# Low parts of the input weights: kept in DRAM after the first pass, loaded again in the second

## The chip, the core and the metric

The kernel runs on one core of one Trainium2 chip, as one program with one launch. Its time is the device time of one execution in microseconds, lower is better; for several executions the median is given. The core has TensorE (PE, matrix products; its weight loads are shown as PEld), VectorE (DVE), ScalarE (ACT), GpSimd (POOL), and SyncE (SP), whose queue issues every DMA of this kernel. Each engine works through its own instructions strictly in the order in which the program issues them, and waits on semaphores for the others.

## The reference, cut to what matters

One inference layer is computed for a prompt of 1024 tokens and for a sample group of 8 x 8 = 64 tokens, with the same weights and in float32:

```
proj = x @ w_in                                  # (tokens, 2048) x (2048, 6672)
conv:  u = glu_a * sigmoid(glu_b); depthwise causal conv, width 31; layer norm; silu; * silu(gate)
delta: q, k, v = silu(conv width 4); gated delta rule, 8 heads x 128, in chunks; rms norm; * silu(gate)
mem:   attention of 4 heads over 256 memory tokens; * silu(gate)
h = concat(conv, delta, mem) @ w_out             # (tokens, 2048) x (2048, 2048)
y = layer_norm(alpha * x + h)
```

The states of the two convolutions, of the delta rule and the memory's keys and values are outputs too.

## The kernel before

**Split products.** A float32 product is made of three fast products (type `fp32r`). A weight block of 128 x 512 arrives in `raw`. ACT copies it into `wh`, rounded to `fp32r`; another engine subtracts, `wl = raw - wh`; the activations are split in the same way into `xh` and `xl`; and PE adds up `wh*xh + wh*xl + wl*xh` in PSUM. One such pair `wh`, `wl` is called a split. `split_quarter` (L302) makes one, half of a `raw` tile, and the kernel makes 592 of them. Which engine subtracts is decided by the number of the split: every second one from the 10th to the 450th goes to POOL, the others to DVE. `wh` and `wl` have four slots each, so a split waits until PE is through with the pair made four splits before it.

**Passes.** `gemm` (L1229) computes one column block of 128 output channels, in four quarters of four contraction blocks; a quarter uses up one split. The first pass runs over 52 column blocks with 576 tokens (half of the prompt and the sample group, in two banks of 288); before block 44 `run_mem` (L1302) computes the memory's keys and values, with 32 splits of its own and, in `load_mem`, eight split activations. The second pass runs over the same 52 blocks and the same weights for the other 512 tokens: it loads them again and splits them again. Then come eight blocks of the output projection with layer norm ("the out stage"), with 144 splits. So the splits are numbered 1 to 240 in the first pass (177 to 208 for the memory), 241 to 448 in the second and 449 to 592 in the out stage.

**Order of the work.** The order of all instructions is written down when the program is made, by a planner. The class `Model` keeps a clock for each engine with a price for each instruction; `Side` holds generators for everything beside the big products: `gen_conv4`, `gen_k`, `gen_q`, `gen_v`, `gen_chain`, `gen_s` for a head of the delta rule (a "unit"), `gen_cgroup` and `gen_cln` for the wide convolution, `gen_att` for a memory head. `side.tick` is called between the products and lets each generator emit a step when its inputs are ready by the model's clock. `side.drain(cond)` emits side work, and no big product, until a condition no longer holds. `ensure(n)` makes splits until `n` of them are ready; it is called with 2 around each quarter.

**What PE may wait for.** In the program's order the subtraction of a split stands between steps of side work on the same engine, and PE takes a `wl` two quarters later.

**POOL's other work** in the passes: in `gen_k` four products of masks, each over 128 x 512 elements (`gmh`, `gml` = triangle times gates; `Dm` = `D` times triangle; `D` times `zn`), in `gen_s` the scaling of the state `S0` (twice) and `ux`, the three sums of `gen_cln`, small copies and powers.

**Work tiles.** Nineteen slots of the tag `W` and sixteen of `T5` hold the intermediate tiles. Nothing in the planner counts them: an instruction that writes a tile for which no slot is free waits on its engine.

**SP's queue.** `load_more` issues loads of `raw` (five slots, 512 KB each) in a fixed sequence; a `raw` slot is free when `done_raw(hi, lo)` says so, that is after the copy and the subtraction of its second half.

## Time and profile before

| what | value |
|---|---|
| median of 3 runs | 2069.68 us (2062.01, 2069.68, 2070.32) |
| the profiled execution | 2062.28 us, its span 2060.6 us |
| PE busy in the span | 1973.7 us (96%) |
| DVE, ACT, POOL busy | 1429.6, 844.7, 605.7 us |
| first pass, memory included | 0 to about 927 us |
| second pass | about 927 to 1649 us |
| out stage | about 1649 to 2060.6 us |
| share of time that the DMA queue's packets take | 36.5% of 16 engines |

The span runs from the first to the last instruction; what lies around it is 1.7 us. The stages are read off the first and last instructions that write the tiles of each stage. Almost all instructions carry the line of one helper (L86), so groups are told apart by the names of their tiles: `wl<-raw,wh` writes `wl` and reads `raw` and `wh`. A busy PE is not a PE at its peak, since matmuls overlap; what counts for the end is the time at which the next big product can start.

### The profile page before, as it was taken

The page shows a single profiled execution, that of the slowest core. Times are in us where ns is not written, and L with a number is a line of the kernel's source. Part 1 is how long each engine was busy: PE and PEld are TensorE (multiplying, and loading weights), DVE is VectorE, ACT ScalarE, POOL GpSimd, SP SyncE. Part 2 cuts the span into 40 slices and gives each one's busy share as a digit, 9 for nine tenths or more (in the row PEclk, how much of TensorE's full clock was granted, in tenths as well). Part 3 has the DMA queues.
Part 4 walks back from the last instruction along what each step waited for, and adds up shares of the span by engine and source line. Part 5 has one row for each costly group of instructions (what it writes and reads, how often), then busy time and mean ns, then how long its engine had stood idle before and what let it go on. Part 6 is the DMA issues. An engine that isn't in the chain of part 4 may idle for free. (4 is left out here: it accounts for less than half of the span.)

```text
span 2060.6 us, 33195 instructions
## 1 busy us (share of the span) xinstructions
PE 1973.7 (96%) x12156; PEld 1708.8 (83%) x12156; DVE 1429.6 (69%) x3190; ACT 844.7 (41%) x2013; POOL 605.7 (29%) x680
## 2 busy tenths in 40 slices
PE   8999999999999989999999999999989999999995
PEld 7999999999999969977777887787767788877784
DVE  7777877887789984255787776779985433348447
ACT  5444444444433345364444444443326522235124
POOL 6434333343323242113333333322322100006003
PEclk9999999999999999999999999999999999999998
DMA  5333233323233355354332223332232563345444
GB/s 205 93 100 93 88 96 102 102 82 99 86 99 97 104 165 167 109 176 149 96 93 89 76 89 104 102 93 82 90 102 92 156 205 105 106 159 182 141 132 144
DMA packets 107267, 239.50 MB, mean 116 GB/s; under 512 B 32224, under 2 KB 36576, under 8 KB 106848
## 3 DMA queue, kind: packets, MB, share of 16 engines
q1 hardware_dynamic: 107104, 237.39, 36.5%
q8 instruction: 95, 1.56, 0.3%
q14 instruction: 68, 0.56, 0.1%
HBM read 210.24 MB, written 27.10 MB: 115 GB/s over the span
## 5 line engine op out<-in xcount | busy, mean ns | idle before, releaser
L86 PE MATMUL m<-xh,wh 128*128 128x288 f32 (+1 forms) x2496 | 860.4, 345 | 7.4 <-ACT wh L86 7.4
L86 PE MATMUL m<-xh,wl 128*128 128x288 f32 (+1 forms) x2496 | 820.1, 329 | 12.7 <-DVE wl L86 9.6
L86 PE MATMUL m<-xl,wh 128*128 128x288 f32 (+1 forms) x2496 | 816.9, 327 | 0.0
L86 ACT CAST wh<-raw 128x512 fp32r<-128x512 f32 x592 | 359.5, 619 | 396.4 <-PE om L86 220.7
L86 POOL TENSOR_TENSOR wl<-raw,wh 128x512 fp32r<-128x512 f32 x221 | 308.5, 1396 | 725.5 <-ACT wh L86 695.5
L86 PEld LDWEIGHTS m<-xh,wh 128*128 128x128 f32 x2496 | 471.0, 189 | 54.3 <-issue 14.1
L86 PEld LDWEIGHTS m<-xh,wl 128*128 128x128 f32 x2496 | 469.7, 188 | 54.3 <-DVE wl L86 14.8
L86 PEld LDWEIGHTS m<-xl,wh 128*128 128x128 f32 x2496 | 471.4, 189 | 29.9 <-issue 2.4
L86 DVE TENSOR_TENSOR wl<-raw,wh 128x512 fp32r<-128x512 f32 x371 | 283.8, 771 | 265.9 <-ACT wh L86 265.5
L86 DVE SCALAR_TENSOR_TENSOR hc<-u,cvc,hc 128x512 f32<-128x512 f32 x360 | 241.5, 713 | 3.1
L86 PE MATMUL om<-wl,xh 128*128 128x512 f32 x576 | 226.8, 394 | 11.6 <-DVE wl L86 10.5
L86 PE MATMUL om<-wh,xh 128*128 128x512 f32 x576 | 226.9, 394 | 4.2 <-ACT wh L86 2.9
L86 PE MATMUL om<-wh,xl 128*128 128x512 f32 x512 | 200.7, 392 | 0.0
L86 DVE TENSOR_TENSOR xt<-mb,X 128x8 f32<-128x8 f32 (+30 forms) x496 | 182.3, 368 | 12.0 <-DVE mb L650 0.3
L86 DVE SCALAR_TENSOR_TENSOR cv<-xr,qcw,cv 128x512 f32<-128x512 f32 (+1 forms) x216 | 167.1, 774 | 7.7
L86 POOL TENSOR_TENSOR y<-y,lnb 128x512 f32<-128x512 f32 (+1 forms) x32 | 51.7, 1639 | 341.7 <-DVE y L86 222.6
L86 PEld LDWEIGHTS om<-wl,xh 128*128 128x128 f32 x576 | 108.9, 189 | 38.8 <-DVE wl L86 14.9
L86 ACT ACT_TABLE_LOAD x89 | 114.2, 1283 | 46.7 <-DVE smz L86 25.8
L86 PEld LDWEIGHTS om<-wh,xh 128*128 128x128 f32 x576 | 109.1, 189 | 29.1 <-ACT wh L86 4.6
L86 DVE TENSOR_REDUCE X<-xt 128x4 f32<-128x8 f32 (+30 forms) x496 | 110.1, 222 | 10.6
L86 PEld LDWEIGHTS om<-wh,xl 128*128 128x128 f32 x512 | 97.1, 190 | 20.2
L86 ACT ACTIVATE oi<-ps,GT 128x128 f32<-128x128 f32 x56 | 20.6, 367 | 207.8 <-DVE r L86 192.7
(309 smaller groups left out, 2010.1 us busy)
## 6 DMA issues: line engine op xcount, KB each, us to landing
raw<-in_wt_dram SPq DMA_DIRECT2D x208, 512.0 KB, 3.8
raw<-in_wo_dram SPq DMA_DIRECT2D x72, 512.0 KB, 3.8
mb<-ysc SPq DMA_DIRECT2D x128, 64.0 KB, 2.2
raw<-mx SPq DMA_DIRECT2D x16, 512.0 KB, 3.8
xt<-in_xp_dram SPq DMA_DIRECT2D x32, 256.0 KB, 4.4
out_y_p_dram<-y SPq DMA_DIRECT2D x32, 256.0 KB, 2.6
xraw<-in_xa_dram SPq DMA_DIRECT2D x16, 288.0 KB, 5.4
S<-in_sdelta_dram SPq DMA_DIRECT2D x16, 256.0 KB, 4.6
```

What stands on the lines that cost most here:

```text
L86: r = fn(**kw)
```

## The change

It does these things:

- In the first pass every `wl` but those of the memory's weights is also written to a DRAM tile of its own (`lop`, 208 of 256 KB); the write is issued by SP one split later.
- In the second pass `wl` isn't computed: after ACT's copy, SP issues a load of the DRAM tile into the `wl` slot. `raw` is then free after ACT's copy alone.
- All other subtractions are on DVE; POOL makes none.
- Five slots for `wh` and `wl` instead of four (`WB`), and `ensure(3)` in `gemm` and `run_mem` instead of `ensure(2)`; the out stage keeps 2 but for its last phase.
- The masks leave POOL: `gmh`, `gml`, `Dz`, `S0` and `ux` are made on ACT, four instructions of 128 columns each (`rscale`). The product `Dm` goes away; in its place PE adds a matrix of -30000 below the diagonal to the exponent (`identr` x `negr`, 512 columns, one for each of 16 units), before ACT's `Exp`.
- The planner counts the slots of `W` and `T5`: generators wait in `room` and `room5` until slots are free (one is kept back for the oldest unit, `fleet[0]`), `need` drains side work until a slot is free, and `finish` drains until the only `xr` buffer has been read (`xbusy`). The sum of squares in `gen_cln` is made with two tiles instead of five. `T5` has 17 slots, the small `Z` tiles 12.
- `xh` and `xl` share one tile.

```diff
+WB = 5
+KEEP = 1
...
-    NW, NX, NU, N5, NZ = 19, 1, 2, 16, 8
+    NW, NX, NU, N5, NZ = 19, 1, 2, 17, 12
...
+    def room(n, last=None):
+        while wfree[0] < n + (0 if last is None or last() else KEEP):
+            yield "B"
+        wfree[0] -= n
...
+    def need(n=1):
+        side.drain(lambda: wfree[0] < n)
...
     def split_quarter():
...
+        n = nsplit[0]
         nsplit[0] += 1
...
         act.copy(out=hi, in_=s)
-        eng = pool if (nsplit[0] % 2 == 0 and 8 < nsplit[0] <= 450) else dve
-        eng.tensor_tensor(out=lo, in0=s, in1=hi.bitcast(F32), op=ALU.subtract)
+        again = n - len(lop) - 32
+        if 0 <= again < len(lop):
+            sp.dma_start(out=lo.bitcast(F32), in_=lop[again])
+        else:
+            dve.tensor_tensor(out=lo, in0=s, in1=hi.bitcast(F32), op=ALU.subtract)
+        while keep and (len(keep) > 1 or keep[0][0] < n - 1 or n >= len(lop) + 32):
+            m, t = keep.popleft()
+            sp.dma_start(out=lop[m], in_=t.bitcast(F32))
+        slot = n if n < 176 else n - 32
+        if n < 176 or 208 <= n < 240:
+            lop[slot] = drp.tile([P, 512], F32, name=f"lo{slot}")
+            keep.append((slot, lo))
...
-            done_raw(hi, lo)
+            done_raw(hi, *(() if 0 <= again < len(lop) else (lo,)))
...
+    def rscale(out, srcs, scales):
+        for c, (x, s) in enumerate(zip(srcs, scales)):
+            act.activation(out=out[:, c, :], in_=x, func=AF.Identity, scale=s)
...
     def gen_k(u):
-        pool.tensor_tensor(out=gmh, in0=bc(triu), in1=bl(gt["gh"][:, 0:4, h].bitcast(F32), 4, P), op=ALU.mult)
-        pool.tensor_tensor(out=gml, in0=bc(triu), in1=bl(gt["gl"][:, 0:4, h], 4, P), op=ALU.mult)
+        yield from room(2, lambda: fleet[0] is u)
+        rscale(gmh, [triu] * 4, [gt["gh"][:, c, h:h + 1].bitcast(F32) for c in range(4)])
+        rscale(gml, [triu] * 4, [gt["gl"][:, c, h:h + 1] for c in range(4)])
...
+        pe.matmul(out=psD.rearrange("p (c n) -> p c n", c=4), lhsT=identr, rhs=bc(negr), start=False, stop=True)
...
-        pool.tensor_tensor(out=Dm, in0=D, in1=bc(triu), op=ALU.mult)
-        u["Dm"] = Dm
-        pool.tensor_tensor(out=D, in0=D, in1=bl(zn, 4, P), op=ALU.mult)
+        u["Dm"] = D
+        rscale(Dz, [D[:, c, :] for c in range(4)], [zn[:, c:c + 1] for c in range(4)])
...
     def finish(p, t, psl):
...
+            side.drain(lambda: xbusy[0])
+            xbusy[0] = 1
             xr, xs = evac_qkv(p, ci, psl)
...
     def gemm(p, t, prev_fin, xhook=None):
-            ensure(2)
+            ensure(3)
```

## The prediction, made before the changed kernel ran

> **What bounds the kernel now.** I read the page's busy times first, then what PE waited for, because PE is the only engine that is nearly full:

> ```profile
> span 2060.6 us, 33195 instructions
> PE 1973.7 (96%) x12156; PEld 1708.8 (83%) x12156; DVE 1429.6 (69%) x3190; ACT 844.7 (41%) x2013; POOL 605.7 (29%) x680
> ```

> The change takes no big product away, so it can only pay where PE stands still or runs slowly. The waits of PE up to 1645 us (both passes), then from 1649 us (the out stage), each as total, number of times and longest in us:

> ```profile
> PE mm L86 <- DVE wl L86: 10.6, 3, 4.6
> PE m L86 <- DVE wl L86: 9.6, 12, 1.7
> PE m L86 <- ACT wh L86: 7.4, 1, 7.4
> PE ps L86 <- DVE rbuf L86: 5.3, 9, 1.2
> PE ps L86 <- DVE S L86: 3.6, 4, 2.0
> PE m L86 <- POOL wl L86: 3.0, 4, 1.1
> PE ps L86 <- DVE ut L86: 2.4, 5, 0.5
> PE ps L86 <- ACT cv L86: 2.2, 2, 1.4
> PE ps L86 <- ACT bdT L86: 1.9, 1, 1.9
> ...
> PE ps L86 <- POOL lsum L86: 1.2, 1, 1.2
> ```

> ```profile
> PE om L86 <- DVE wl L86: 10.5, 6, 6.8
> PE om L86 <- ACT wh L86: 2.7, 1, 2.7
> ```

> The reader is to see how little there is. Late subtractions in the passes cost 10.6 + 9.6 + 3.0 = 23.2 us; side work adds some 17; the 7.4 is the start, and the 13.2 lie in the out stage, whose splits are on DVE before and after. The three waits at `mm` (the memory's products) cost more than themselves. The next table cuts the span where the granted clock fell; its columns are stretch, length, busy us (instructions) of PE, PEld, DVE, ACT, POOL, the granted clock, DMA share and GB/s:

> ```profile
> 720.40:723.80 3.40, 3.40 (x10) 2.63 (x9) 3.40 (x9) 0.62 (x1) 0.00 (x0) 0.50 0.83 272
> 737.50:740.90 3.40, 3.40 (x10) 2.66 (x9) 3.40 (x9) 0.84 (x2) 0.00 (x0) 0.51 1.00 329
> 754.50:757.90 3.40, 3.40 (x9) 2.66 (x9) 3.40 (x6) 0.62 (x1) 0.72 (x1) 0.50 0.86 227
> 914.90:921.70 6.80, 6.80 (x20) 5.55 (x20) 2.15 (x12) 5.67 (x10) 0.00 (x0) 0.50 0.13 54
> ```

> Behind each of them PE ran 3.4 us at half clock and lost 1.7 us: 5.1 us. The fourth, 6.8 us long, stands behind the wait for `bdT`, the gates of the second pass.

> The chain that ended last gives the price of a big product of 512 columns where nothing holds it up, 200.39 / 871 = 0.23 us:

> ```profile
> 1648.95 200.39 PE om L86 x871
> ```

> **The change part by part.** *Splits on DVE and DRAM.* What a subtraction costs, in ns (min/median/max, first and last start), and its busy us in three stretches (PE, PEld, DVE, POOL):

> ```profile
> L86 DVE TENSOR_TENSOR wl<-raw,wh x371: 628/691/1928, 7.4 to 2032.9; 128x512 fp32r<-128x512 f32 x186
> L86 POOL TENSOR_TENSOR wl<-raw,wh x221: 1260/1296/1852, 40.8 to 1641.8; 128x512 fp32r<-128x512 f32 x111
> ```

> ```profile
> 581.00:742.00 161.00, 104.49 (x340) 64.56 (x340) 19.25 (x27) 41.45 (x28) 0.98 0.33 107
> 720.00:772.00 52.00, 23.31 (x55) 11.62 (x55) 12.93 (x14) 19.42 (x13) 0.90 0.52 165
> 1649.00:2033.00 384.00, 217.87 (x555) 104.82 (x555) 102.26 (x142) 0.00 (x0) 0.99 0.45 148
> ```

> With POOL splitting too, one on DVE takes 12.93/14 = 0.92 us around the memory; with POOL at none, 102.26/142 = 0.72. By the split's number POOL made (240 - 10)/2 + 1 = 116 in the first pass and 105 later. After it, DVE makes 240 + 144 = 384 instead of 371, and of those 116 more in the first pass: 116 x 0.72 = 84 us there; in the second it loses 104.

> The first pass has one stretch without room, the wide convolution. Engines there (PE, PEld, DVE, ACT, POOL), then its steps on DVE (the shape 128x64, mean 434 ns) and the shortest of both its shapes (268 ns):

> ```profile
> 581.00:742.00 161.00, 154.99 (x1116) 148.41 (x1115) 156.42 (x299) 49.33 (x104) 47.90 (x41) 0.98 0.33 107
> ...
> L86 DVE SCALAR_TENSOR_TENSOR hc<-u,cvc,hc 128x64 f32<-128x64 f32 x113 | 49.0, 434 | 0.0
> ```

> ```profile
> L86 DVE SCALAR_TENSOR_TENSOR hc<-u,cvc,hc x360: 268/740/1826, 583.0 to 1532.2; 128x512 f32<-128x512 f32 x180
> ```

> DVE has 161 - 156.4 = 4.6 us free and gets 28 x 0.72 = 20.2 us. If the steps of 64 fall from 434 to 268 ns once POOL is quiet, 113 x 0.166 = 18.8 us come back, so it just closes. The planner also charges a DVE split to the model's clock, and `gen_cgroup` stops when DVE is 1200 ns ahead, so convolution steps move later, not the splits; from 742 us on DVE is less full. And a third split lies ready, which is one quarter more of slack. Of the 23.2 us between 0 and all go; I take four fifths, **-18.6 us**, since the waits are short (longest 4.6) against a quarter of 12 products of 0.23 us = 2.8 us. With the waits at `mm` the three half-clock stretches go: **-5.1 us** (0 at the other end).

> [...] Here three waits of together 10.6 us were each followed by half clock, so at least one of them was no longer than 3.6. [...]

> *Loads in the second pass.* SP issues 208 stores and 208 loads more, of 256 KB. Its issue time, and the loads of that size that are slowest to land (median 5.8 us):

> ```profile
> L86 SPq DMA_DIRECT2D raw<-in_wt_dram x208: 327/328/1592, 1.7 to 1598.1; - x104
> ```

> ```profile
> vts<-in_cv_dram SPq DMA_DIRECT2D x16, 256.0 KB, 5.8
> ```

> 416 x 0.33 = 137 us of a queue that mostly waits. Split j+3 takes the slot of j-2, free when quarter j-1 begins, and is used from j+3: four quarters, 11.0 us, less 5.8 leaves 5.2 us. Hidden, 0; the other end is a rival. What stands before a load in SP's queue is what DVE, ACT and POOL have still to finish for another DMA.

> *End of the second pass.* `raw` is free without the subtraction. The chain that ended last has it on the path:

> ```profile
> 1630.99 1.39 POOL wl L86
> 1632.39 5.94 DMA raw<-mx
> ```

> **-1.4 us** (0 to -1.4; the loads behind it stay).

> *Masks.* POOL's products end, the longest of them 1.36 us each; ACT makes each with four instructions that are nearest to this one (387 ns), and PE adds 16 products that are nearest to `gml`'s (6.4 us busy in all, 398 ns each):

> ```profile
> L86 POOL TENSOR_TENSOR Dm<-D,triu 128x512 f32<-128x512 f32 x16 | 21.7, 1355 | 0.0
> ```

> ```profile
> L86 ACT ACTIVATE ot<-ot,oz x64: 385/387/404, 171.1 to 1447.3; 128x128 f32<-128x128 f32 x64
> ```

> ```profile
> L86 PE MATMUL ps<-gml,trilr 128*128 128x512 f32 x16 | 6.4, 398 | 0.0
> ```

> ACT: 16 units x 12 + 8 x 12 = 288 instructions, 111 us on 845, a share of 46%. A mask takes 1.55 us instead of up to 1.36, and `A` no longer waits for `Dm`; big products hide it, so 0. Without that cover one mask late in each unit is 16 x 1.55 = 25 us. PE: between 16 x 0.23 = 3.7 and 6.4 us, on the path; in a stream the start-to-start time counts, **+3.7 us**.

> *Side work on DVE.* Waits for `rbuf`, `S`, `ut` are 11.3 us. These small steps wait behind larger ones that POOL slows. Between 0 and -11.3 I take a third, **-3.8 us**.

> *The ledger.* `room`, `need` and `xbusy` move side work in the program's order. Where slots never run out this costs nothing. Nothing in the trace counts slots; one wait the size of `bdT`'s is my value, **+1.9 us** (from 0 to the 66 us of the third rival). The out stage, its one extra slot included: 0, since it still makes two splits ahead.

> Sum: -18.6 - 5.1 - 1.4 + 3.7 - 3.8 + 1.9 = -23.3 us. The profiled execution took 2062.3, of which the span is 2060.6; so **2039 us**. That execution is at the low end of the runs (2062.0, 2069.7, 2070.3); the 7.4 us to their median may or may not come again, and I leave them to the range.

> **The rivals.** *All waits of the passes go* (0.17). For it: DVE and POOL are in nearly all of them. All rows of the first fence but the start are 39.8 us, half clock 5.1 + 3.4, the slot 1.4, the mask 3.7: 2062.3 - 39.8 - 8.5 - 1.4 + 3.7 = 2016. Against: the chains of small products keep their round trips.

> *DVE becomes the bound of the convolution and of the memory stage* (0.17). If POOL's quiet brings nothing back, DVE is 20.2 - 4.6 = 15.6 us over in the convolution and 13 x 0.72 = 9.4 us more around the memory; 25 us eat the gain: 2064, no change. Against: 0.72 against 0.92.

> *The ledger empties* (0.11), the slower side. In both passes' ends the attention holds its tiles while gates and queries of four heads each ask for slots through `need`; a drain emits a head's softmax with no big product between, and PE waits for its round trip, as in this part of the chain, 1564.49 to 1568.62:

> ```profile
> 1564.49 0.70 DVE smz L86
> ...
> 1565.46 1.28 ACT L86
> 1566.75 1.03 ACT pt L86 x4
> ...
> 1568.01 0.61 DVE pt L86 x2
> ```

> 4.1 us; 16 such drains are 66 us: 2039 + 66 = 2105. From six on (6 x 4.1 = 25) it decides the sign. Against: in the trace these stages ran with the same nineteen slots and PE hardly waited.

> *Loads come late* (0.10). SP's longest wait in the second pass for something that stays:

> ```profile
> SPq L86 <- POOL xr L86: 29.3, 10, 5.2
> ```

> 5.2 us is just what is left. If half of 104 pairs of splits came 0.8 us late, 42 us: 2081. From 23 us on, that is 29 such pairs, it cancels the gain. [...]

> **How the numbers follow.** My forecast has 0.45, the rivals 0.17, 0.17, 0.11 and 0.10. Its own range is 2025 (-23.2 - 5.1 - 1.4 + 3.7 - 11.3 = -37.3, the ledger at 0) to 2057 (half of the first two terms, the dear end of the mask, nothing from side work: -9.3 - 2.6 - 1.4 + 6.4 + 1.9 = -5.0). The range for 8 in 10 is 2006 to 2078: below, 2016 and some of the doubt about a third of the waits that I counted as fixed; above, the no-change case with the 7.4 us between runs, and some of the late loads; the ledger's case stays outside. Half a per cent, 10 us, is about what a measurement of this kernel can tell from none. Faster: 0.45 + 0.17 and a little of the second rival, 0.64; the same: 0.17; slower: 0.19.

> **What would show it.** Right: the waits of `mm` and `m` for `wl` shrink below 5 us in all; no half clock between 700 and 780 us; DVE's `wl` close to 0.72 us in the first pass; the second pass has no DVE or POOL `wl` and no PE wait for its load; SP's waits stay under 5.2 us. Wrong: PE waiting on DMA for `wl` (late loads); stretches where only `ps` products run and PE idles between them (ledger); DVE at 100% with PE behind `wl` from 580 to 770 us (DVE); a time under 2016 would mean that big products gain from something that I didn't find.

## The result, and the profile after

The changed kernel takes 2029.28 us (median of 2028.79 to 2029.90), the kernel before 2067.28 us beside it (2062.01 to 2070.32): a ratio of 0.982, 95% interval 0.980 to 0.984, or 38 us less. The profiled execution of the changed kernel took 2028.79 us, 33.5 us less than that of before (2062.28). The forecast was 2039, a fall of 23.3 us.

The page of the changed kernel begins so:

```profile
span 2026.3 us, 33634 instructions
PE 1961.8 (97%) x12172; PEld 1708.4 (84%) x12172; DVE 1262.3 (62%) x3203; ACT 925.6 (46%) x2298; POOL 192.3 (9%) x373
```

PE's 16 more products are those that make the mask. POOL fell from 605.7 to 192.3 us, and DVE fell too, by 167 us, though it makes 13 subtractions more. Next the waits of PE, up to 1613 us and in the out stage (total, times, longest in us):

```profile
PE m L88 <- DMA wl<-lo: 6.1, 4, 2.1
PE ps L88 <- DVE rbuf L88: 3.4, 2, 2.1
PE bd L88 <- DMA raw<-in_xb_dram: 3.3, 2, 2.9
PE ps L88 <- DVE ut L88: 3.3, 4, 1.3
PE mm L88 <- DVE wl L88: 2.9, 3, 1.4
...
PE m L88 <- DVE wl L88: 0.8, 1, 0.8
...
PE ps L88 <- DVE S L88: 0.5, 1, 0.5
```

```profile
PE om L88 <- DVE wl L88: 8.6, 3, 7.0
```

The waits for a subtraction in the passes went from 23.2 to 3.7 us. Two kinds are new: 6.1 us for a low part that is still on its way from DRAM, and 3.3 us for the second pass's inputs (`raw<-in_xb_dram`), at 887 and 891 us, just ahead of that pass.

Where the time came from shows in a cut by stages. The bounds are the starts of PE's first product of the passes, the first of the memory (`mm`), the last of the memory, the first one of 512 columns (second pass), the first and the last of the out stage (`om`). Columns: stretch, length, busy us (instructions) of PE, PEld, DVE, ACT, POOL, granted clock, DMA share, GB/s. Before, then after:

```profile
7.40:711.40 704.00, 695.59 (x5622) 672.33 (x5623) 569.21 (x1503) 299.19 (x815) 263.55 (x352) 1.00 0.32 101
711.40:772.90 61.50, 50.89 (x197) 39.88 (x196) 53.70 (x82) 25.44 (x44) 30.21 (x20) 0.92 0.51 165
772.90:908.40 135.50, 135.06 (x987) 119.41 (x985) 52.97 (x95) 66.49 (x137) 25.85 (x20) 1.00 0.50 155
908.40:1637.70 729.30, 704.46 (x3688) 563.07 (x3686) 538.66 (x1192) 318.86 (x792) 223.77 (x221) 1.00 0.32 99
1637.70:2040.80 403.10, 387.39 (x1668) 314.07 (x1668) 200.25 (x299) 126.78 (x216) 46.96 (x33) 0.99 0.46 150
```

```profile
7.30:717.00 709.70, 698.02 (x5631) 673.69 (x5632) 527.06 (x1548) 355.77 (x1007) 82.39 (x214) 1.00 0.53 166
717.00:765.20 48.20, 45.26 (x193) 35.71 (x193) 48.20 (x99) 23.28 (x40) 0.00 (x0) 1.00 0.62 200
765.20:892.00 126.80, 122.19 (x894) 112.60 (x892) 68.73 (x128) 56.20 (x114) 9.40 (x6) 1.00 0.63 210
892.00:1613.00 721.00, 712.52 (x3793) 572.70 (x3792) 404.16 (x1114) 357.64 (x914) 39.24 (x87) 1.00 0.57 180
1613.00:2006.20 393.20, 383.40 (x1669) 313.72 (x1667) 197.75 (x296) 124.70 (x214) 43.88 (x32) 0.99 0.47 153
```

The lengths differ by +5.7, -13.3, -8.7, -8.3 and -9.9 us; with the ends, -34.3 us of span. Four things are to be seen. The first pass got *longer*. The memory stage gained most for its size, with DVE busy in all of its 48.2 us and PE waiting for 2.9. Side work moved: of the small products (`ps` and `bd`) 124 stand in the tail of the first pass instead of 216, and 1294 in the second pass instead of 1190. From the start of each to the next start, waits left out, they take 11.1 us less in the tail and 13.1 us more in the second pass. So all of the tail's gain is moved work, and the second pass gained in spite of it: PE stands still there for 8.5 us instead of 24.8 (length less busy time). And the out stage, of which nothing was expected, gave 9.9 us.

The start of the out stage, in the chain that ended last (start, length, what), before and after:

```profile
1641.86 4.54 DMA raw<-mx
...
1648.39 0.52 ACT wh L86
...
1648.95 1.22 PE om L86 x2
```

```profile
1613.15 12.07 PE om L88 x53
```

and its first 14.5 us in both, columns as above, before and after:

```profile
1637.70:1648.80 11.10, 7.50 (x28) 4.94 (x28) 6.86 (x17) 7.05 (x19) 1.45 (x1) 1.00 0.70 246
1648.80:1652.20 3.40, 3.25 (x8) 2.53 (x9) 3.10 (x5) 1.66 (x4) 0.00 (x0) 0.50 0.78 229
```

```profile
1613.00:1624.00 11.00, 11.00 (x50) 9.10 (x49) 8.92 (x21) 7.43 (x21) 0.00 (x0) 1.00 0.78 256
1624.00:1627.50 3.50, 3.50 (x17) 2.89 (x16) 1.29 (x2) 1.01 (x2) 0.00 (x0) 1.00 0.91 232
```

Before, PE began 36 products there, with stops and then at half clock; after, 64 without a stop (the rows count three more, because a product that crosses a bound is counted on both sides). 28 products of 0.23 us are 6.4 of the 9.9 us.

DVE's steps got faster with POOL quiet. Groups before and after (busy us, mean ns); `hc` is the convolution's step of 64 columns, and `xt` mixes 31 widths from 8 to 128 columns:

```profile
L86 DVE SCALAR_TENSOR_TENSOR hc<-u,cvc,hc 128x64 f32<-128x64 f32 x120 | 53.0, 442 | 0.0
L86 DVE TENSOR_TENSOR xt<-mb,X 128x8 f32<-128x8 f32 (+30 forms) x496 | 182.3, 368 | 12.0 <-DVE mb L650 0.3
```

```profile
L88 DVE TENSOR_TENSOR wl<-raw,wh 128x512 fp32r<-128x512 f32 x384 | 267.9, 710 | 201.1 <-ACT wh L88 185.2
L88 DVE SCALAR_TENSOR_TENSOR hc<-u,cvc,hc 128x64 f32<-128x64 f32 x120 | 35.3, 294 | 0.0
L88 DVE TENSOR_TENSOR xt<-mb,X 128x8 f32<-128x8 f32 (+30 forms) x496 | 137.6, 277 | 11.1
```

### The profile page after: what moved, and what is told of

The parts are those of the page before. It is cut to its first block, busy times and chain, and to the rows that moved or that the text cites. A ratio compares the mean times of both kernels' runs of the same rounds, so it can differ in the third digit from the quotient of the medians.

```text
span 2026.3 us, 33634 instructions
## 1 busy us (share of the span) xinstructions
PE 1961.8 (97%) x12172; PEld 1708.4 (84%) x12172; DVE 1262.3 (62%) x3203; ACT 925.6 (46%) x2298; POOL 192.3 (9%) x373
## 4 chain that ended last, share of the span: by engine, by line
PE 44%; DVE 4%; ACT 1%; DMA 1%; POOL 1%; issue 1%; SPq 0%; DVEq 0%; ACTq 0%; POOLq 0%
PE m L88 23%; PE om L88 17%; PE ps L88 5%; DVE y L88 2%; DVE cv L88 1%; DVE wl L88 1%; DMA wl<-lo 0%; POOL y L88 0%; ACT wh L88 0%; DMA xsc<-X 0%; SPq L88 0%; DVE xt L88 0%; ACT jk L88 0%; DVE X L88 0%; ACT gmh L88 0%
## 5 line engine op out<-in xcount | busy, mean ns | idle before, releaser
L88 PE MATMUL m<-x,wh 128*128 128x288 f32 (+1 forms) x4992 | 1228.9, 336 | 7.5 <-ACT wh L88 7.3
L88 PEld LDWEIGHTS m<-x,wh 128*128 128x128 f32 x4992 | 831.7, 189 | 83.1 <-issue 17.1
L88 PE MATMUL m<-x,wl 128*128 128x288 f32 (+1 forms) x2496 | 818.6, 328 | 6.8 <-DMA wl<-lo 6.1
L88 PEld LDWEIGHTS m<-x,wl 128*128 128x128 f32 x2496 | 469.6, 188 | 44.2 <-DMA wl<-lo 8.6
L88 PE MATMUL om<-wh,x 128*128 128x512 f32 x1088 | 342.6, 391 | 1.2 <-DVE y L88 1.2
L88 PEld LDWEIGHTS om<-wh,x 128*128 128x128 f32 x1088 | 205.0, 189 | 45.2 <-DVE y L88 1.6
L88 PE MATMUL om<-wl,x 128*128 128x512 f32 x576 | 225.7, 392 | 8.6 <-DVE wl L88 8.6
L88 DVE TENSOR_TENSOR xt<-mb,X 128x8 f32<-128x8 f32 (+30 forms) x496 | 137.6, 277 | 11.1
L88 PEld LDWEIGHTS om<-wl,x 128*128 128x128 f32 x576 | 108.7, 189 | 32.9 <-DVE wl L88 10.3
L88 DVE SCALAR_TENSOR_TENSOR cv<-xr,qcw,cv 128x512 f32<-128x512 f32 (+1 forms) x216 | 129.3, 599 | 7.7
L88 DVE SCALAR_TENSOR_TENSOR y<-xt,om 128x512 f32<-128x512 f32 (+1 forms) x36 | 24.1, 683 | 31.9 <-PE om L88 30.0
## 6 DMA issues: line engine op xcount, KB each, us to landing
lo<-wl SPq DMA_DIRECT2D x208, 256.0 KB, 4.8
wl<-lo SPq DMA_DIRECT2D x208, 256.0 KB, 4.0
xt<-in_xp_dram SPq DMA_DIRECT2D x32, 256.0 KB, 4.5
out_y_p_dram<-y SPq DMA_DIRECT2D x32, 256.0 KB, 2.6
```

The lines of the kernel that those rows point to most:

```text
L88: r = fn(**kw)
```

## The experiments

Stage lengths of all kernels, in us, between the same starts of products as above (F first pass to the memory, M memory, T tail of the first pass, S second pass, O out stage), with the ratio to the kernel before on the same chip:

| kernel | F | M | T | S | O | median | ratio (95%) |
|---|---|---|---|---|---|---|---|
| before | 704.0 | 61.5 | 135.5 | 729.3 | 403.1 | 2067.3 | 1 |
| after | 709.7 | 48.2 | 126.8 | 721.0 | 393.2 | 2029.3 | 0.982 (0.980 to 0.984) |
| e12, after again | 711.4 | 48.1 | 126.6 | 724.2 | 393.7 | 2032.2 | 0.9842 (0.9827 to 0.9856) |
| e1 | 712.4 | 46.6 | 125.4 | 744.5 | 401.5 | 2060.3 | 0.9985 (0.9976 to 0.9995) |
| e10 | 705.6 | 46.4 | 123.3 | 748.9 | 393.3 | 2043.7 | 0.9907 (0.989 to 0.9924) |
| e14 | 713.0 | 48.2 | 124.3 | 746.3 | 393.7 | 2054.9 | 0.9948 (0.9934 to 0.9961) |
| e2 | 727.7 | 49.7 | 130.7 | 733.2 | 401.0 | 2068.9 | 1.0013 (0.9999 to 1.0027) |
| e8 | 732.7 | 60.6 | 132.5 | 740.8 | 394.4 | 2086.6 | 1.0113 (1.009 to 1.0136) |
| e7 | 711.2 | 48.0 | 124.3 | 720.3 | 391.5 | 2025.3 | 0.9818 (0.9801 to 0.9835) |
| e3 | 713.5 | 60.1 | 134.4 | 706.7 | 392.6 | 2035.5 | 0.9862 (0.9845 to 0.9879) |
| e4 | 720.2 | 47.6 | 128.2 | 704.3 | 393.3 | 2024.3 | 0.9816 (0.9801 to 0.9831) |
| e13, e4 again | 722.1 | 47.7 | 128.5 | 704.5 | 393.3 | 2025.1 | 0.9805 (0.9791 to 0.9818) |
| e15 | 710.5 | 48.3 | 126.5 | 724.1 | 393.3 | 2030.9 | 0.9831 (0.9818 to 0.9845) |
| e11 | 724.8 | 47.5 | 128.0 | 707.3 | 391.7 | 2028.1 | 0.9825 (0.9806 to 0.9844) |

e1 to e4 shared one chip, e7, e8, e10 and e11 another, e12 to e15 a third.

**e1: the second pass subtracts on DVE; nothing is stored or loaded.**

```diff
-        again = n - len(lop) - 32
+        again = -1
...
-        while keep and (len(keep) > 1
+        while False and keep and (len(keep) > 1
...
-        if n < 176 or 208 <= n < 240:
+        if False:
```

> The changed kernel (2029 us) without the stores and loads of low parts: DVE makes all subtractions of the second pass too. Theory (the loads take load off a full DVE): the 6.1 us in which PE waits for loaded low parts and the 1.7 us of half clock behind one of them go, but DVE gets 208 x 0.69 = 143 us more in the second pass and PE waits for it again in the wide convolution and at the start of the out stage, about as before the change (11.8 us and 5 us): 2034 to 2040 us. Rival (quiet POOL and the third split ahead give the whole gain, the loads give nothing): the load waits go and nothing comes instead, 2018 to 2024 us.

2060.25 us (2058.01 to 2062.86). Neither theory had that. PE in the order of time (start, length, product, idle before and what ended it):

```profile
1053.73 1.69 PE L88 MATMUL ps<-kts,dgq 128*32 128x256 f32 x16
1058.65 0.69 PE L88 MATMUL ps<-ident,pt 128*128 128x128 f32 x2 [3.23 <-DVE pt L88]
1072.29 1.08 PE L88 MATMUL ps<-vts,ptm 128*32 128x256 f32 x8 [12.96 <-DVE ptm L88]
```

No big product stands between 1053.8 and 1074 us, and from 1057.5 to 1078.0 PE is at half clock. In this kernel's order a drain of side work stands there: DVE makes 22 of the 31 steps of the loop in `gen_k` that inverts a triangular block row by row (`xt`, 1058.5 to 1071.9 us), and only then the copy `ptm` for which PE waits. That DVE's extra price in the model's clocks shifted the order until the slots ran out is inferred from the code and from e10, where the drain is gone; no trace counts slots. This is the mechanism of the prediction's third rival, which the changed kernel itself doesn't show. The run therefore doesn't price the loads alone, and e10 was made.

**e10: as e1, but the planner's clocks are advanced as if the stores and loads were there** (`ghost`), so that ACT, POOL and, the subtractions left out, DVE work in the changed kernel's order, as the traces show, and no drain happens.

```diff
-            sp.dma_start(out=lo.bitcast(F32), in_=lop[again])
+            nc.vector.tensor_tensor(out=lo, in0=s, in1=hi.bitcast(F32), op=ALU.subtract)
+            ghost(lo, ("lop", again))
...
-            sp.dma_start(out=lop[m], in_=t.bitcast(F32))
+            ghost(("lop", m), t)
```

> As e1_dve2 (no stores, no loads, DVE subtracts in the second pass), but the planner is told the clocks of the changed kernel, so that all other work keeps the changed kernel's order and the ledger holds. Theory (the loads relieve a DVE that is too full): the load waits of 6.1 us and 1.7 us of half clock go, PE waits for DVE's low parts again in the wide convolution and at the start of the out stage, 8 to 16 us: 2030 to 2040 us. Rival (e1_dve2 lost its time in drains of the ledger alone; with a quiet POOL and a third split ahead, DVE needs no relief): second pass 712 to 722 us, the whole 2018 to 2030 us.

2043.67 us (2042.03 to 2047.42), above both theories. 16.6 us of e1's loss were the order (the two ran on different chips, on which the kernel before differs by 0.9 us). The second pass is 27.9 us longer than with loads, and everything ahead of it 9.4 us shorter. Of PE's waits here, these stand in the second pass:

```profile
PE ps L88 <- POOL lsum L88: 4.2, 1, 4.2
PE m L88 <- DVE wl L357: 3.9, 5, 1.4
```

The subtraction itself (`wl`) is waited for 3.9 us only; most of the rest of the loss is in waits for side work, of which `lsum` is the largest, and in half clock (13.7 us at 1178.4).

**e14: e10 with the 208 stores issued** (the first pass is then that of the changed kernel, the second that of e10; the edit is shown against e10).

```diff
-            ghost(("lop", m), t)
+            sp.dma_start(out=lop[m], in_=t.bitcast(F32))
```

> The second pass subtracts on DVE, in the order of e10, but the first pass now does issue its 208 stores. Theory, the stores cost the changed kernel its 9 us before the second pass: the first pass 709 to 711 us (705.6 without them), memory stage and tail together 173 to 175 (169.7), second pass 748 to 750 as in e10, in all 2050 to 2054. Rival, it is the loads' side (their place in SP's queue, the reserve of slots) that shifts the stages before: 705 to 707 and 169 to 171, in all 2042 to 2047.

2054.90 us (2052.96 to 2055.71); beside it e12, the changed kernel, 2032.18. The first pass is 713.0 long against e10's 705.6, memory and tail 172.5 against 169.7. These 10.2 us are the theory's stores (its total was missed by 0.9 us, its three stages by 0.5 to 2.0), with a reserve: e10 ran on another chip, and the changed kernel's first pass differs by 1.7 us between two chips. How a store comes to cost PE time shows in one place of e14 (SP's issues, DVE, PE):

```profile
346.60 4.90 SPq L88 DMA_DIRECT2D mb<-ysc  x8
351.55 0.58 SPq L88 DMA_DIRECT2D lo<-wl  x1
354.19 0.69 DVE L88 TENSOR_TENSOR wl<-raw,wh 128x512 fp32r<-128x512 f32 x1 [4.44 <-DMA lo<-wl]
355.25 0.67 PE L88 MATMUL ps<-rbuf,Y 64*64 64x64 f32 x8 [2.27 <-DVE rbuf L88]
```

A `wl` slot can't be written again before its store has landed, here at 354.09 us. SP issues this store behind eight small loads, so DVE stands still for 4.44 us, `rbuf` behind it is late, PE waits for 2.27 us, and 6.8 us of half clock follow. In e10 the same step of DVE waits 0.48 us, and PE doesn't wait. In all, DVE waits for stores 8 times, 15.2 us. Over the first pass PE stands still for 4.0 us more than in e10 (11.9 against 7.9), and the half clock costs 3.4: that is the 7.4 us.

On one chip, e14 against e12 gives the loads' worth: 746.3 against 724.2 in the second pass, 22.1 us, and 22.7 in all. Of the 22.1, 14.1 are PE's idle time (24.1 against 10.0) and 1.7 half clock; the rest isn't put down to anything. In e14 PE waits there for `wl` (4.0 us), for DVE's small steps `xt`, `ptm`, `ut`, `Rc`, `pt`, `rbuf` and `S` (12.0 together) and for POOL's `lsum` (4.2); in e12 for late loads (7.7) and hardly for the others.

**e2: four slots, two splits ahead, all else changed.**

```diff
-WB = 5
+WB = 4
...
-ensure(3)
+ensure(2)
```

> The changed kernel with four slots and two splits ahead, as before the change. Theory (a third split ahead is worth a third of the gain): waits for loads double to about 14 us, memory stage and out stage lose 3 to 6 us each: 2036 to 2046 us. Rival (look-ahead gives the whole gain): back to 2055 us or more. Second rival (look-ahead gives nothing, a quiet POOL all): 2027 to 2031 us.

2068.90 us (2063.31 to 2071.59): the whole gain is gone. The largest of PE's waits:

```profile
PE m L88 <- DMA wl<-lo: 17.7, 10, 3.7
```

With one quarter less between issue and use, ten loads are late instead of four; the out stage is back at 401.0; and the first pass, which loads nothing, is 18 us longer, and 13 half-clock stretches stand between start and end of the execution, against 2 in the changed kernel (4 in e12). In the first pass DVE waits 30.3 us for slots whose store hasn't landed, against 15.1: with four slots instead of five a slot is needed again sooner. PE stands still there for 22.5 us instead of 11.7, for small steps of the chains (`Us` 4.7 us, `ot` 4.0) rather than for splits, and half clock costs 8.5 us instead of nothing. That these steps are late because of the stores is likely after e14, but wasn't followed wait by wait. So e2 doesn't undo the look-ahead alone: it also makes the stores dearer.

**e8: the kernel before with three splits ahead and five slots, POOL unchanged, nothing stored** (`xh` and `xl` share a tile, to make room).

```diff
+WB = 5
...
-            ensure(2)
+            ensure(3)
```

> The kernel before with five slots and three splits ahead, and with xh and xl in one tile to make room; POOL still splits and masks. Theory (POOL's slowness and the look-ahead share the gain): memory stage 61 to about 56 us, second pass 8 to 10 us shorter, out stage 5 to 10: 2042 to 2052 us. Rival (look-ahead gives the whole gain): 2026 to 2036 us. Second rival (it gives nothing without a quiet POOL): 2060 us or more.

2086.64 us (2082.50 to 2090.91), slower than before, as only the second rival had it. The memory stage keeps its waits:

```profile
PE mm L87 <- DVE wl L87: 10.0, 3, 4.9
```

but the out stage falls to 394.4 us. With e2 (loads, but two ahead: 401.0) and e10 (no loads, but three ahead: 393.3) this names what gave the out stage its 9.9 us: one split more that lies ready when the second pass ends. As the first `om` product starts, two splits of the out stage are finished in the changed kernel, e10 and e8, one in e2, and in the kernel before not even the first. Three ahead in the code isn't enough by itself: e1 has it too, but there ACT came to these splits so late that PE waited 3.4 us for the first, and the out stage is 401.5 us. Why both passes of e8 get longer (732.7 and 740.8) is open; nothing is stored here, and more look-ahead shifts every later step of the order.

**e7: loads issued on ACT's queue instead of SP's, and three ahead in all of the out stage.**

```diff
-            sp.dma_start(out=lo.bitcast(F32), in_=lop[again])
+            act.dma_start(out=lo.bitcast(F32), in_=lop[again])
...
-                ensure(3 if last else 2)
+                ensure(3)
```

> The changed kernel with two edits: the loads of low parts are issued by ACT, behind its own copy of the same split, instead of by SP; and the out stage keeps three splits ahead instead of two. Theory (SP holds the loads up, since it waits in order for DVE; the out stage has too few splits ahead): waits for loads fall from 6.1 us to under 2 and with them a half-clock stretch, second pass 721 to about 714 us; the out stage's longest wait of 7 us loses a split's 2.8 to 3.2 us and its first ones as much, 393 to about 387: 2014 to 2022 us in all. Rival (loads are late because the DMA engines are full, and the out stage waits for layer norm): 2026 to 2031 us.

2025.31 us (2023.53 to 2029.13), between the two theories. No wait for a low part's load is left, so its place in SP's queue was what made it late. But the second pass gains 0.7 us:

```profile
PE ps L88 <- DVE xt L88: 2.8, 1, 2.8
```

Other waits took the place (2.5 us more for `kts`), and a half-clock stretch of 6.8 us stands at 1184.5. The ratio is the changed kernel's.

**e3: POOL makes every second subtraction of the first pass again.**

```diff
-            dve.tensor_tensor(out=lo, in0=s, in1=hi.bitcast(F32), op=ALU.subtract)
+            eng = pool if (n % 2 == 1 and 8 < n < 240) else dve
+            eng.tensor_tensor(out=lo, in0=s, in1=hi.bitcast(F32), op=ALU.subtract)
```

> The changed kernel, in the first pass every second subtraction on POOL again. Theory (POOL and DVE hinder each other, and a subtraction on POOL is late): the memory stage goes from 48 back to about 58 us with its half-clock stretches, 2038 to 2046 us. Rival (look-ahead covers it): memory stage 48 to 50 us, 2028 to 2032 us.

2035.51 us (2031.67 to 2036.90). The memory stage is back at 60.1 us, with its waits:

```profile
PE mm L88 <- DVE wl L88: 9.5, 4, 4.9
```

and half clock (6.8 us at 744.0). The planner ordered other work anew too, but the stage doesn't follow the order: the three kernels in which POOL splits (before, e8, e3) have 60.1 to 61.5 us there, the eleven others 46.4 to 49.7. So POOL's splits beside DVE's are the cause. DVE is busy in nearly all of the stage in both, for 59.6 us with 86 instructions in e3 and 48.2 with 99 in the changed kernel: it has less to do and takes longer. In all e3 is less than the theory's 2038 to 2046, because the second pass came out at 706.7 instead of 721.0; 72 products fewer stand in it, and 70 more in the tail.

**e4: the masks, the scaling of `S0` and `ux` on POOL again, one product of 512 columns each** (`pool.tensor_tensor` for `rscale`; the mask product on PE stays).

```diff
-        rscale(Dz, [D[:, c, :] for c in range(4)], [zn[:, c:c + 1] for c in range(4)])
+        pool.tensor_tensor(out=Dz, in0=D, in1=bl(zn, 4, P), op=ALU.mult)
```

> The changed kernel with the five masks of a unit made by POOL in one instruction each instead of by ACT in four; the product of the mask on PE stays. Theory (POOL's masks slow DVE by holding it up): the small products wait a little longer, 3 to 6 us: 2032 to 2035 us. Rival (masks are hidden on either engine): 2027 to 2031 us.

2024.28 us (2022.77 to 2027.89): below both theories. The first pass is 10.5 us longer than the changed kernel's, the second 16.7 shorter.

**e12 and e13: the changed kernel and e4 on one chip.**

> The changed kernel once more, unaltered, so that the three others have it on their own chip. Both theories: 2027 to 2031 us, ratio to the kernel before 0.980 to 0.984, whatever the chip; if it lies outside, differences of a few us between kernels run on different chips mean nothing.

> The masks, the state scaling and the outer-product tiles on POOL in both passes, beside the changed kernel on one chip. If the 4.5 us between the two medians of different chips are real: 2022 to 2026 and 3 to 6 us below the changed kernel here. Rival, chance of the chip (the ratios to the kernel before were 0.9816 and 0.982): within 2 us of the changed kernel.

2032.18 us (2030.14 to 2036.56) and 2025.13 (2024.13 to 2026.06): on one chip e4 is faster by 7.1 us, and the intervals of the two ratios, 0.9842 and 0.9805, lie apart. On their first chips they were 0.982 and 0.9816, which told nothing. The changed kernel lies a hair outside what was expected of it, so differences of some 3 us between chips mean nothing here. Of e13's waits:

```profile
PE ps L88 <- DVE r L88: 6.6, 5, 2.3
PE ps L88 <- DVE ut L88: 6.1, 6, 1.9
...
PE m L88 <- DMA wl<-lo: 0.6, 1, 0.6
```

The chains of the first pass wait for `r` and `ut`, and the late loads of the second pass are nearly gone.

**e15: only the second pass makes `gmh`, `gml` and `Dz` on POOL** (`if p:` around e4's lines).

```diff
-        rscale(Dz, [D[:, c, :] for c in range(4)], [zn[:, c:c + 1] for c in range(4)])
+        if p:
+            pool.tensor_tensor(out=Dz, in0=D, in1=bl(zn, 4, P), op=ALU.mult)
+        else:
+            rscale(Dz, [D[:, c, :] for c in range(4)], [zn[:, c:c + 1] for c in range(4)])
```

> Only the second pass makes its masks (gmh, gml, Dz) on POOL; the first pass, the state scaling and the outer products stay as changed. Theory, what a stage gains by it is that stage's own (with all masks on POOL the second pass was 16.7 us shorter, the first 10.6 longer): first pass 709 to 711, second 704 to 712, in all 2012 to 2020. Rival, the second pass of that kernel gained because the longer first pass had taken side work from it (side products 112.5 us in the second pass of the changed kernel, 104.7 there): second pass 716 to 722, in all 2024 to 2030.

2030.94 us (2028.08 to 2032.49): near the rival, 0.9 us above its range. The second pass is 724.1 us, as in e12, though ACT has 96 instructions fewer, and the loads are as late as ever:

```profile
PE m L88 <- DMA wl<-lo: 9.4, 5, 3.7
```

So e4's gain in the second pass isn't that of its masks there. The second pass of e13 is 19.7 us shorter than e12's: 8.3 us of small products (from start to next start) are made earlier, in the first pass and its tail; PE stands still for 3.2 us instead of 10.0, with 0.6 us of late loads instead of 7.7; and two half-clock stretches are gone, 3.4 us. Which of the moved instructions starts it is open.

**e11: e7 and e4 together.**

```diff
+            act.dma_start(out=lo.bitcast(F32), in_=lop[again])
...
+        pool.tensor_tensor(out=Dz, in0=D, in1=bl(zn, 4, P), op=ALU.mult)
...
+                ensure(3)
```

> e7_both with the masks on POOL as in e4_poolmask (2024 us, where the second pass was 17 us shorter and the first 11 us longer than in the changed kernel). Theory (the three gains add): 2010 to 2018 us. Rival (e4_poolmask's gain is the luck of another order, and goes once the order changes again): 2016 to 2026 us.

2028.06 us (2025.13 to 2029.87), above both theories. The two don't add up: the first pass is 724.8 us, and without late loads to save, nothing is won behind it. The lowest ratio of the study is that of e13 (e4 again), 0.9805.

Not tried: the kernel before with all subtractions on DVE and nothing else changed, and the fifth slot without the third split ahead.

## Why the prediction was right, and where it was not

The time lies in the forecast's own range, 10 us below its number. The late subtractions were right in size and cause, the half clock in cause. That the rest came out so close is in part luck: some 16 us of loads and stores that the sum put at nothing stand against an out stage and a second pass that gained more than it had. Step by step:

| step | forecast | measured |
|---|---|---|
| late subtractions in the passes | -18.6 | -19.5 (23.2 to 3.7) |
| half clock | -5.1 | -8.5 (27.2 us of stretches to 10.2, half of it lost) |
| loads in the second pass | 0 | +6.1 for `wl` |
| the second pass's inputs (`raw<-in_xb_dram`) | not in the sum | +3.3, at the end of the tail |
| stores in the first pass | 0 | about +10 (e14 against e10) |
| mask on PE | +3.7 | +3.7 (the 16 products, from start to next start) |
| side waits (`rbuf`, `S`, `ut`) | -3.8 | -4.1 (11.3 to 7.2) |
| ledger | +1.9 | -1.9 (`bdT` no longer waited for, no drain in which PE stands still) |
| `raw` free earlier, out stage | -1.4 and 0 | -9.9 |

The rows don't add up to the result, and should not: the stores' price is made of waits and moved work that other rows hold too, and some of the difference lies in time that the records call busy.

*The step that failed is the out stage*, put at 0 "since it still makes two splits ahead". It does, but it starts with what the second pass leaves, and that is one split more than before. The chain before had two transfers `raw<-mx` of 5.94 and 4.54 us with a wait for `wh` behind them; the prediction quoted the first, took 1.4 us for the subtraction ahead of it, and wrote that the loads stay. They stayed, but were no longer on the path. e8, e10 and e2 show that this needs the look-ahead of three in the second pass, and that the stores and loads don't give it; e1 shows that the look-ahead must also be made in time.

*Late subtractions*: right in size and cause (e3). DVE's price was put at 0.72 us and is 0.71. The convolution closes as worked out: between 581 and 742 us DVE is busy for 143.2 of 161 us, with 55 subtractions instead of 27; its steps of 64 columns take 285 ns (put at 268). The rival "DVE becomes the bound" falls. What the sum left out is that the gain in the second pass isn't only the subtractions that PE waited for. e14 against e12 prices the absence of 208 subtractions at 22.1 us there, while the waits for `wl` that they cause are 4.0 us (e14); the small steps that share DVE with them hold PE up for longer.

*Side waits*: the -4.1 is a difference. The second pass lost all of its 7.0 us of waits for `S`, `ut` and `rbuf`, and the first pass rose from 4.5 to 7.2. Both passes have a quiet POOL, which was the cause that the prediction gave. What sets them apart is that DVE has no subtractions left in the second pass and has stores to wait for in the first; e14, whose second pass subtracts, has 4.0 us of these waits again.

*Half clock*: the three stretches around the memory went, as forecast, and so did those behind `bdT` and at 1648.8; one came, behind a late load. The grid on which they lie is told below.

*Loads and stores* were put at nothing, the loads with a rival at 0.10. Sizes and landing times in the changed kernel (KB, median us), then the late load for which PE waited longest (SP's issues, PE):

```profile
lo<-wl SPq DMA_DIRECT2D x208, 256.0 KB, 4.8
wl<-lo SPq DMA_DIRECT2D x208, 256.0 KB, 4.0
```

```profile
1171.36 4.90 SPq L88 DMA_DIRECT2D mb<-ysc  x8
1176.36 0.53 SPq L88 DMA_DIRECT2D wl<-lo  x1
1179.33 0.61 PE L88 MATMUL m<-x,wl 128*128 128x512 f32 x1 [2.15 <-DMA wl<-lo]
```

A load lands in 4.0 us, not 5.8, so the transfer had 7.0 us of slack instead of 5.2. Four came late all the same, and each had landed within 3.0 us of its issue. What held them up is the queue, as e7 shows, and there a small tile's round trip through DRAM: ahead of this load SP waits 2.0 us until `ysc` is written and then issues eight loads of it in 4.9 us; ahead of the next late one it waits 3.7 us for `xsc`. The two others stand behind such a trip as well. The prediction looked at SP's longest wait for another engine, and in the second pass that stayed under its 5.2 us (4.9 at most, apart from up to 7.9 for ACT's copies `wh`). A wait for a DMA and the time of eight issues were not in its sum. The rival's mechanism is real and its size was 6.1 us with a half-clock stretch, not 42; PE waiting on DMA for `wl` was also one of the prediction's own signs of being wrong. The stores have no wait of their own on PE, and the prediction costed only their issue on SP. They hold up DVE, by slots that aren't free yet (15.1 us in 8 times here, 15.2 in e14), and through its small steps PE.

*Mask and masks*: ACT makes a mask in 4 x 391 ns, as worked out, and PE's 16 products are busy 391 ns each. The move to ACT was put at 0, hidden by big products. e13, with the same masks on POOL, is 7.1 us faster, and e15, with those of the second pass alone, 1.2 us, which is no difference. So the move gained nothing by itself. e13's first pass is 10.7 us longer than e12's and its second 19.7 shorter, so what the move costs lies in how the order falls behind it.

*Ledger*: without price in the changed kernel; in e1 the same ledger cost one wait of 13 us and the half clock around it.

*The parts belong together.* Undoing the look-ahead and its fifth slot costs the whole gain (e2); the look-ahead alone makes the kernel before 1.1% slower (e8). A sum of steps with fixed prices can't show that.

## What to carry to other kernels

Look at what a stage inherits from the one before: one more operand ready at a boundary took two transfers off the path, in a stage whose own code was unchanged. Where an order is planned by a model's clocks, undo a part with the model's clocks held fixed (e10), since else the reordering (16.6 us from e1 to e10) is taken for the part's price. And moving a result through DRAM instead of computing it again has two prices beside its gain: here 22 us won where it is loaded, about 10 lost where it is stored, since a slot stays taken until its store has landed (15.1 us of DVE's waits), and a place in an in-order queue that decides whether the load is in time (6.1 us of PE's waits).

## What the runs showed of the hardware

```profile
1176.19:1179.60 3.41, 1.26 (x6) 0.76 (x5) 2.52 (x9) 1.14 (x2) 0.19 (x1) 1.00 0.80 201
1179.60:1183.01 3.41, 3.41 (x9) 2.63 (x9) 0.00 (x0) 0.00 (x0) 0.00 (x0) 0.50 0.47 165
1869.10:1872.51 3.41, 1.58 (x7) 0.97 (x6) 3.36 (x2) 0.62 (x1) 3.41 (x3) 1.00 0.83 315
1872.51:1875.92 3.41, 0.00 (x0) 0.00 (x0) 1.97 (x3) 0.00 (x0) 2.29 (x2) 1.00 0.42 156
```

PE stood still for 2.15 us of the first, and the next window is at half clock, with PE busy in all of it. It stood still for 1.83 us of the third (1.79 by the records' unrounded times), and the fourth was granted the full clock, though PE did nothing in it. Over the 14 profiles, start and end left out, all of the 70 windows with 2.0 us or more of idle were followed by half clock; between 1.5 and 2.0 us 20 were and 22 weren't; below 1.5 us, of some 8000, 22 were, and 21 of these carried on a stretch that had begun. The traces of the kernels before and after have 7 of the 70, and of the windows between 1.5 and 2.0 us 3 that were followed and 7 that weren't. One longer wait fell on a bound of the grid: after the change PE waits 2.88 us for `raw<-in_xb_dram`, up to 891.03 us; 1.28 us of it lie before the bound at 889.43 and 1.60 behind it, and the clock stayed full in both windows and in the next. So a wait of over 2 us cost 1.7 us more (the 2.15 us ahead of 1179.60) or nothing (these 2.88), by where it fell on the grid.

*DVE was slower while POOL worked.* In the trace of the kernel before, the 254 subtractions on DVE during which POOL had no instruction running took 686 ns on average, and the 117 that met one took 954; of the convolution's steps of 64 columns, 92 without took 273 ns and 28 that met one 997. With POOL at 9% instead of 29%, the 496 `xt` steps went from a mean of 368 to 277 ns (rows above), and they alone gave 45 us of DVE time. e3, with POOL's splits back in the first pass alone, shows what of it lies on the path: 11.9 us in the memory stage.
